# Layer 0's output projection by seven half-size products with positions as rows, in a two-layer mLSTM and gated-attention trunk

## The chip, the cores and the metric

The kernel runs on one core of a Trainium2 chip. The metric is the device time of one execution in microseconds (us). The core's engines each work through a queue of their own in order: TensorE (PE; its weight loads are listed as PEld), VectorE (DVE), ScalarE (ACT), GpSimd (POOL), and SyncE (SP), which here only issues DMAs.

## The reference

512 positions of width 1024 go through two layers, each `x <- x + RMSNorm_post(mixer(RMSNorm_pre(x)))`. Layer 0's mixer is an mLSTM with 4 heads of width 512, layer 1's a gated linear attention with 4 heads. Cut to what matters here:

```python
for i in range(DEPTH):                        # DEPTH = 2
    h = rms_norm(x, pre_norm_w[i])
    out = mlstm_mixer(h, ...) if i == 0 else gla_mixer(h, ...)
    x = x + rms_norm(out, post_norm_w[i])
# the end of mlstm_mixer: y is (512, 2048), w_out is (2048, 1024)
y = (hn * norm_w + skip * uc) * silu(z)
return y @ w_out
```

## The kernel before

Activations lie with channels on the 128 partitions and the 512 positions along the free axis; a tile `t2` is 128x512 float32, and 59 buffers of that size are shared by all of them. Every large product is made in three matmuls: both operands are split into a high part (float32r, a copy by ScalarE) and a low part (the difference, by VectorE), and high x high, high x low and low x high are added up in PSUM. `mm` (L123) issues all matmuls, `split` (L138 high, L139 low) all splits, so the profile is read by tile names.

Weights come in chunks of 128x1024, one DMA on SP's queue into one of three `raw` buffers, then a split into `whi` and `wlo` (four buffers each). `run_jobs` writes out the program: for each job it first forms the chunks of the jobs up to `LA` = 3 ahead, then runs what `later` has put off to this job, then pops `n` entries of the list `steps` (VectorE and ScalarE work spread over the jobs) and `b` of `spare`, and then issues the job's matmuls and what follows them. No planner reorders it: each engine's queue has the order in which this loop comes to its instructions.

Layer 0 has four heads. For head h the weighted scores `S` and values `VS` give the numerators (`m_num`: den and four num banks), then `m_scale`, `m_skip` (GpSimd), `m_rstd` and `m_y` finish y, and `y_split` splits it. The output projection follows: `out_full` and `out_job` take one block of 128 output channels at a time as the stationary side and positions as the moving side, in two halves of 256 positions; eight blocks x two halves x 16 blocks of y x 3 = 768 matmuls of 256 columns. Half 0 is finished first; `residual` then makes its norm factor by a matmul with ones and adds x, `x1_done` applies layer 1's input weight and splits the result into `ghi2` and `glo2`, and a `turn` of four TensorE transposes per pair of blocks stores x1 by rows for the end of the kernel. Layer 1's first five products (`kept_a` for half 0, `kept_b` for half 1) run while half 1's residual steps go on. Since x1 isn't normed yet, every evacuation in layer 1 multiplies by `rs1` or `rcol` (`pre_rstd`, `rstd_columns`).

Layer 1's own output projection is already made of seven half-size products P1 to P7 (Winograd's form of Strassen's method): positions are the stationary side in blocks of 128, 512 output channels the moving side. Its sums of weight blocks U, W, Z and R are made in DRAM by 32 DMAs of GpSimd's queue, `combine` makes the sums of y blocks, and 336 matmuls of 512 columns do the work. P3 and P7 come already split from DRAM (`PRE`).

## Time and profile before

| | |
|---|---|
| runs before | 917.6 us median of 3 (916.42 to 917.76) |
| the profiled execution | 917.5 us, its span 915.8 us |
| TensorE busy | 902.4 us (99%), 4624 matmuls |
| VectorE, ScalarE, GpSimd busy | 630.6, 523.3, 183.2 us |
| mean granted TensorE clock | 0.996 of full |
| DMA | 147.58 MB, mean 161 GB/s |

The span runs from the first to the last instruction of the core. Busy times of matmuls overlap, since one starts before the record of the one in front has ended; VectorE's and ScalarE's overlap by less.

### The profile page before, as it was taken

The page shows a single profiled execution, that of the slowest core. Times are in us where ns is not written, and L with a number is a line of the kernel's source. Part 1 is how long each engine was busy: PE and PEld are TensorE (multiplying, and loading weights), DVE is VectorE, ACT ScalarE, POOL GpSimd, SP SyncE. Part 2 cuts the span into 40 slices and gives each one's busy share as a digit, 9 for nine tenths or more (in the row PEclk, how much of TensorE's full clock was granted, in tenths as well). Part 3 has the DMA queues.
Part 4 walks back from the last instruction along what each step waited for, and adds up shares of the span by engine and source line. Part 5 has one row for each costly group of instructions (what it writes and reads, how often), then busy time and mean ns, then how long its engine had stood idle before and what let it go on. Part 6 is the DMA issues. An engine that isn't in the chain of part 4 may idle for free. (4 is left out here: it accounts for less than half of the span.)

```text
span 915.8 us, 12449 instructions
## 1 busy us (share of the span) xinstructions
PE 902.4 (99%) x4624; PEld 760.7 (83%) x4624; DVE 630.6 (69%) x916; ACT 523.3 (57%) x885; POOL 183.2 (20%) x162
## 2 busy tenths in 40 slices
PE   9999999999999999999999999999999999999995
PEld 6887878878877888899999997777888888888874
DVE  5999797886886668788658746743346547478854
ACT  6865685756654558866557626544435345365642
POOL 0022552262250043245002310421000000000121
PEclk9999999999999999999999999999999999999998
DMA  8334344352342223222775694995343736383776
GB/s 309 120 122 147 117 151 137 116 169 97 123 142 69 93 70 115 92 93 69 232 235 198 206 323 166 236 243 140 116 138 114 242 115 200 118 287 104 269 275 138
DMA packets 50882, 147.58 MB, mean 161 GB/s; under 512 B 5792, under 2 KB 10272, under 8 KB 50528
## 3 DMA queue, kind: packets, MB, share of 16 engines
q1 hardware_dynamic: 44832, 120.29, 39.7%
q0 software_dynamic: 5696, 26.22, 10.8%
q8 instruction: 38, 0.62, 0.3%
q14 instruction: 28, 0.23, 0.1%
q10 hardware_dynamic: 288, 0.22, 0.1%
HBM read 129.92 MB, written 34.60 MB: 180 GB/s over the span
## 5 line engine op out<-in xcount | busy, mean ns | idle before, releaser
L139 DVE TENSOR_TENSOR wlo<-raw,whi 128x1024 fp32r<-128x1024 f32 (+1 forms) x146 | 186.3, 1284 | 98.8 <-ACT whi L138 98.1
L138 ACT CAST whi<-raw 128x1024 fp32r<-128x1024 f32 (+1 forms) x146 | 149.9, 1036 | 79.0 <-PE gv L123 24.2
L394 POOL TENSOR_TENSOR vp<-V,wv 128x512 f32<-128x512 f32 x56 | 88.6, 1604 | 177.4 <-ACT V L482 92.6
L123 PE MATMUL op<-yhi,whi 128*128 128x256 f32 x256 | 73.5, 287 | 0.0
L123 PE MATMUL op<-yhi,wlo 128*128 128x256 f32 x256 | 72.5, 283 | 0.4 <-DVE wlo L139 0.4
L123 PE MATMUL op<-ylo,whi 128*128 128x256 f32 x256 | 72.8, 284 | 0.0
L397 DVE SCALAR_TENSOR_TENSOR vp<-V,wv 128x512 f32<-128x512 f32 x72 | 68.0, 987 | 0.0
L163 POOL DMA_DIRECT2D whi<-wpP x8 | 4.3, 536 | 244.7 <-DMA raw<-in_w_gout 216.9
L123 PE MATMUL gz<-g2h,whi 128*128 128x512 f32 x128 | 51.5, 403 | 0.5 <-PEq L1156 0.5
L123 PEld LDWEIGHTS op<-ylo,whi 128*128 128x128 f32 x256 | 49.1, 192 | 1.1 <-DVE ylo L139 0.6
L123 PE MATMUL gz<-g2h,wlo 128*128 128x512 f32 x128 | 49.9, 390 | 0.0
L123 PE MATMUL gz<-g2l,whi 128*128 128x512 f32 x128 | 49.8, 389 | 0.0
L123 PE MATMUL qk<-chi,whi 128*128 128x512 f32 x128 | 49.8, 389 | 0.0
L123 PE MATMUL qk<-chi,wlo 128*128 128x512 f32 x128 | 49.8, 389 | 0.0
L123 PE MATMUL qk<-clo,whi 128*128 128x512 f32 x128 | 49.8, 389 | 0.0
L123 PE MATMUL gv<-whi,g2h 128*128 128x512 f32 x128 | 49.8, 389 | 0.0
L123 PE MATMUL gv<-wlo,g2h 128*128 128x512 f32 x128 | 49.8, 389 | 0.0
L123 PE MATMUL gv<-whi,g2l 128*128 128x512 f32 x128 | 49.8, 389 | 0.0
L123 PEld LDWEIGHTS op<-yhi,wlo 128*128 128x128 f32 x256 | 49.1, 192 | 0.6 <-DVE wlo L139 0.6
L123 PEld LDWEIGHTS op<-yhi,whi 128*128 128x128 f32 x256 | 49.1, 192 | 0.5 <-issue 0.5
L123 PE MATMUL z<-hhi,whi 128*128 128x512 f32 x112 | 44.1, 394 | 0.0
L123 PE MATMUL z<-hlo,whi 128*128 128x512 f32 x112 | 43.7, 390 | 0.0
(286 smaller groups left out, 2503.9 us busy)
## 6 DMA issues: line engine op xcount, KB each, us to landing
raw<-in_w_min SPq DMA_DIRECT2D x30, 512.0 KB, 3.7
raw<-in_w_mout SPq DMA_DIRECT2D x29, 512.0 KB, 4.2
wv<-in_wgv SPq DMA_DIRECT2D x32, 256.0 KB, 3.6
raw<-in_w_qk SPq DMA_DIRECT2D x16, 512.0 KB, 3.7
raw<-in_w_gqk SPq DMA_DIRECT2D x16, 512.0 KB, 4.0
raw<-in_w_gz SPq DMA_DIRECT2D x16, 512.0 KB, 5.2
raw<-in_w_gv SPq DMA_DIRECT2D x16, 512.0 KB, 4.1
raw<-in_w_v SPq DMA_DIRECT2D x8, 512.0 KB, 3.5
```

Source lines behind the costliest of these rows:

```text
L123: nc.tensor.matmul(out, lhsT=lhsT, rhs=rhs, start=start, stop=stop, skip_group_check=more)
L138: nc.scalar.copy(hi, src)
L139: nc.vector.tensor_sub(lo, src, hi.bitcast(F32))
L163: nc.gpsimd.dma_start(to, of)
L394: nc.gpsimd.tensor_mul(j, V[h][i], w)
L397: nc.vector.scalar_tensor_tensor(j, V[h][i], 1.0, w, op0=ALU.mult, op1=ALU.mult, accum_out=o)
```

## The change

Layer 0's output projection is made like layer 1's. A class `Seven` holds the seven products for both (`m7` for layer 0, `g7` for layer 1, whose code is moved into it). Layer 0's weight sums are made by 32 DMAs that GpSimd issues during the q and k products of heads 1 to 3. y of heads 0 and 1 is split as the first operand and saved to DRAM (`ysave`), and loaded again for the combines. Positions are now rows: the post-norm's sum of squares is a free-axis accumulation on ScalarE, the residual comes from x by rows (`xrows`), `h_rows` applies layer 1's input norm by rows, and TensorE turns the normed rows (`turn`) into `ghi2` and `glo2`. As layer 1's input is normed by then, its evacuations lose their multiply: q and k are copied by ScalarE, z goes straight from PSUM into the activation. For head 3 the square sums move from GpSimd to VectorE; `m_skip` stands ahead of `m_num`. Layer 0's products all come as raw chunks (`DMA_LOW` is empty, so the "dma" kind isn't used). The weights of the low-rank gate load earlier, in the same order of jobs.

```diff
+    class Seven:
+        TO = {"P1": "a", "P6": "a", "P7": "a", "P4": "a", "P5": "c", "P3": "c", "P2": "d"}
...
+        def sum_start(self, n, c):
+            w = self.w
+            nc.gpsimd.dma_start(self.wsum[n, c], {"U": w[1, 0, c], "W": w[0, 0, c], "Z": w[0, 1, c], "R": w[0, 0, c]}[n])
+        def sum_add(self, n, c):
+            w, ws = self.w, self.wsum
+            nc.gpsimd.dma_start(ws[n, c], {"U": w[1, 1, c], "W": ws["U", c], "Z": ws["W", c], "R": w[1, 0, c]}[n],
+                                accum_op=ALU.add, max_dma_last_dim=4096)
...
+        def first_operand(self, k, y):
+            nc.vector.tensor_sub(y[:, self.b], y[:, self.a], y[:, self.b])
+        def combine(self, k):
+            y1, y2 = self.Y[0, k], self.Y[1, k]
+            a, b = self.a, self.b
+            for to, x, y in ((y1[:, b], y1[:, b], y2[:, b]), (y1[:, a], y1[:, b], y1[:, a]),
+                             (y2[:, a], y1[:, b], y2[:, a])):
+                nc.vector.scalar_tensor_tensor(to, x, -1.0, y, op0=ALU.mult, op1=ALU.subtract)
+        def operand4(self, c):
+            self.ops["4", c] = t2("yhi", F32R), t2("ylo", F32R)
+            for i in range(2):
+                split(*(z[:, HALF[i]] for z in self.ops["4", c]), self.Y[1, 2 * c + i][:, self.a])
...
+        def product(self, name, chunks, tb, c0=0):
+            to = self.TO[name]
+            if (to, tb) not in self.bank:
+                self.bank[to, tb] = psum("op")
+            ps = self.bank[to, tb]
+            more = name in ("P6", "P7", "P4", "P3")
+            for c, (whi, wlo) in enumerate(chunks):
+                for i in range(2):
+                    k = 2 * (c0 + c) + i
+                    yh, yl = (z[:, tb * P:(tb + 1) * P] for z in self.block(name, k))
+                    mm(ps, yh, whi[i], k == 0 and not more, False, more)
+                    mm(ps, yh, wlo[i], False, False, more)
+                    mm(ps, yl, whi[i], False, k == 7, more)
...
+        def out_part(self, r, m, to, name, tb):
+            self.parts[r, m] = t2("o")
+            nc.vector.tensor_add(self.parts[r, m], self.bank[to, tb], self.sums[name, tb])
+            self.part_sum(r, m, self.parts[r, m])
...
+    m7, g7 = Seven("m", w_mout, 0), Seven("g", w_gout, 1, PRE)
...
+    m_sums = sums_of(m7)
+    def next_sums(n):
+        for _ in range(n):
+            if m_sums:
+                m_sums.pop(0)()
     A = [None] * NH
     V = [None] * NH
     st = {}
@@ -517,6 +690,7 @@
                     gate_add(wgr[:, 16 * which + n, :], *d[n])
             later(2 if h else 3, gates)
+            next_sums(3 if h else 0)
...
-                nc.gpsimd.tensor_add(sqs[0], sqs[0], sqs[vt])
+                (nc.vector if h == NH - 1 else nc.gpsimd).tensor_add(sqs[0], sqs[0], sqs[vt])
...
-            if vt < 2:
-                load_uc(n + 2)
-            nc.gpsimd.tensor_mul(zs[n], st["uc", n], zs[n])
+            nc.gpsimd.tensor_mul(st["uc", n], st["uc", n], zs[n])
...
+    ysave = dp.tile([8, P, T], F32, name="ysave")
+    def y_out(h, vts):
         for vt in vts:
-            n = 4 * h + vt
-            yhi[n], ylo[n] = t2(f"yhi{n}", F32R), t2(f"ylo{n}", F32R)
-            split(yhi[n], ylo[n], HC[h][vt])
+            n, y = 4 * h + vt, HC[h][vt]
+            if h < 2:
+                m7.first_operand(n, y)
+                m7.operand("1", n, y)
+                nc.sync.dma_start(ysave[n], y)
+            else:
+                m7.Y[1, n - 8] = y
+                m7.operand("2", n - 8, y)
+    def load_y(k):
+        m7.Y[0, k] = t2("yr")
+        nc.sync.dma_start(m7.Y[0, k], ysave[k])
...
+        if h == NH - 1:
+            job(lambda: [load_y(k) for k in range(4)], n=0)
+        job(lambda h=h: (m_skip(h), m_num(h), m_scale(h)), n=0)
...
-                for n in range(2):
-                    out_full(n)
+                for c in range(2):
+                    m7.job("P1", c)
+                    m7.job("P5", c)
...
+    def x1_rows(r):
+        c = m7.row_rstd(r)
+        for m in range(2):
+            o = m7.parts[r, m]
+            nc.vector.scalar_tensor_tensor(o, o, c, m7.pw[:, m * T:(m + 1) * T], op0=ALU.mult, op1=ALU.mult)
+        for m in range(2):
+            o = m7.parts[r, m]
+            nc.vector.tensor_add(o, o, m7.res[r, m])
+            m7.part_sum(r, m, o, ssx)
+            nc.sync.dma_start(x1_d[r, :, m * T:(m + 1) * T], o)
+    def h_rows(r):
+        c = m7.row_rstd(r, ssx, rsx1)
+        for m in range(2):
+            hrow[r, m] = t2("hr")
+            nc.scalar.activation(hrow[r, m], m7.parts[r, m], AF.Copy, scale=c)
...
+    def turn(kp, half):
         sl = HALF[half]
+        ps = psum("xt")
         for i in range(2):
             k = 2 * kp + i
+            for j in range(2):
+                nc.tensor.transpose(ps[:, (2 * i + j) * P:(2 * i + j + 1) * P],
+                                    hrow[2 * half + j, k // 4][:, k % 4 * P:(k % 4 + 1) * P], ident)
...
+            of, w = ps[:, HALF[i]], col(PV_PRE + 8 + k)
+            nc.scalar.activation(ghi2[k][:, sl], of, AF.Identity, scale=w)
+            nc.vector.scalar_tensor_tensor(glo2[k][:, sl], of, w, ghi2[k][:, sl].bitcast(F32),
+                                           op0=ALU.mult, op1=ALU.subtract)
...
+    def m_after_p7():
+        for tb in range(2):
+            m7.out_part(tb, 1, "a", "e5", tb)
+        later(1, lambda: (x1_rows(0), x1_rows(1)))
+        later(2, lambda: (h_rows(0), h_rows(1)))
...
+    job(lambda: (m7.load_pw(0), steps.extend(pairs(m7.combine, (0, 2)))), n=0)
+    DK = lambda name, c: "dma" if (name, c) in DMA_LOW else "ring"
+    m7.job("P5", 2)
+    job(lambda: (head_steps(NH - 1), [load_y(k) for k in range(4, 8)], steps.extend(
+        pairs(m_op3, (0,)) + [lambda v=v: (m_y(NH - 1, (v, v + 1)), y_out(NH - 1, (v, v + 1))) for v in (0, 2)]
+        + pairs(m_op3, (2,)) + pairs(m7.combine, (4, 6)) + pairs(m_op3, (4, 6))
+        + [lambda c=c: m7.operand4(c) for c in range(4)]
+        + [lambda: None, lambda: gla_weights(0, 0)] + [lambda: None] * 6
+        + [lambda i=i: gla_weights(i // 2 + 1, i % 2) for i in range(4)])), n=0)
+    for name, c in (("P5", 3), ("P1", 2), ("P1", 3), ("P3", 0), ("P3", 1), ("P2", 0), ("P2", 1), ("P6", 0), ("P6", 1),
+                    ("P3", 2), ("P3", 3), ("P6", 2), ("P6", 3), ("P2", 2), ("P7", 0), ("P7", 1)):
+        m7.job(name, c, kind=DK(name, c))
+    job(lambda: [m7.load_res(r, rows_of_x) for r in (0, 1)], n=0)
+    for name, c in (("P7", 2), ("P7", 3), ("P2", 3)):
+        m7.job(name, c, la=LA + (name == "P2"), kind=DK(name, c))
+    job(lambda: [m7.load_res(r, rows_of_x) for r in (2, 3)], n=0)
+    def m_last(r):
+        m7.parts[r, 1] = t2("o")
+        nc.vector.tensor_copy(m7.parts[r, 1], m7.bank["a", r - 2])
+        m7.part_sum(r, 1, m7.parts[r, 1])
+    for c in range(4):
+        m7.job("P4", c, n=2, kind="t2r" if c > 1 else "ring")
+    for kp in range(4):
+        job(lambda kp=kp: turn(kp, 0), n=0, la=0)
+    job(lambda: (m_last(2), x1_rows(2), m7.product("P4", m7.last, 1)), n=8)
...
-        return lambda: nc.vector.tensor_mul(raw[j][:, sl], ps, rs1[:, sl])
+        return lambda: nc.scalar.copy(raw[j][:, sl], ps)
...
-    job(lambda: pre_rstd(0), n=0)
-    kept_a(*head[0], "keep")
-    job(lambda: (rstdB(), steps.extend([lambda k=k: addB(k) for k in range(KP + 2)])), n=0)
+    kept_a(*head[0], "keep", 4)
+    job(lambda: (m_last(3), x1_rows(3), h_rows(2)), n=0)
     kept_a(*head[1], "keep")
+    job(lambda: h_rows(3), n=0)
     kept_a(*head[2], "keep2")
-    job(lambda: low_rank(0), n=2)
+    job(lambda: low_rank(0))
     kept_a(*head[3], "keep2", 1)
     kept_a(*head[4], "keep2", 0)
     job(lambda: low_rank_evac(0), n=8, la=0)
+    for kp in range(4):
+        job(lambda kp=kp: turn(kp, 1), n=0, la=0)
+    kept_b(*head[0])
     job(lambda: low_rank(1), la=0)
-    kept_b(*head[0])
-    job(lambda: pre_rstd(1))
+    kept_b(*head[1])
```

## Rows read from the trace of the kernel before

**Rows 1.** Windows: stretch, busy PE, PEld, DVE, ACT, POOL, clock, DMA, GB/s.

```profile
541.00:637.00 96.00, 95.48 (x408) 74.83 (x407) 52.88 (x97) 47.52 (x68) 19.34 (x34) 1.00 0.81 216
828.00:906.00 78.00, 77.37 (x340) 63.10 (x339) 56.58 (x95) 40.24 (x74) 12.09 (x20) 1.00 0.64 200
```

**Rows 2.** Waits of TensorE, whole span: us in total, times, longest.

```profile
PE op L123 <- DMA wlo<-wpP: 0.6, 1, 0.6
```

**Rows 3.** Tile op (both layers' outputs): count, ns min/median/max, first and last start.

```profile
L123 PE MATMUL op<-yhi,whi x256: 277/283/683, 396.7 to 500.6; 128*128 128x256 f32 x128
...
L123 PE MATMUL op<-whi,yhi x96: 388/389/793, 828.0 to 894.5; 128*128 128x512 f32 x96
```

**Rows 4.** Timeline of TensorE, layer 0's output stage: start, us, instruction, [idle before].

```profile
396.72 0.68 PE L123 MATMUL op<-yhi,whi 128*128 128x256 f32 x1
...
408.63 0.39 PE L123 MATMUL den<-shi,csr 128*128 128x512 f32 x1
...
417.52 0.33 PE L123 MATMUL op<-yhi,whi 128*128 128x256 f32 x1
...
501.38 1.13 PE L123 MATMUL ssq<-sq,cs 128*128 128x256 f32 x4 [0.21 <-POOL sq L310]
502.34 0.60 PE L898 MATMUL xt<-cs,o 128*128 128x128 f32 x4
```

**Rows 5.** Timeline of TensorE, layer 1's output stage.

```profile
839.40 0.79 PE L123 MATMUL op<-whi,yhi 128*128 128x512 f32 x1
840.04 0.40 PE L123 MATMUL op<-wlo,yhi 128*128 128x512 f32 x1
...
905.89 0.39 PE L123 MATMUL op<-khi,ylo 128*128 128x512 f32 x1
```

**Rows 6.** Timeline of VectorE around the start of layer 0's output.

```profile
404.84 1.29 DVE L739 TENSOR_TENSOR hc<-hc,z 128x512 f32<-128x512 f32 x2
406.05 1.22 DVE L139 TENSOR_TENSOR wlo<-raw,whi 128x1024 fp32r<-128x1024 f32 x1
407.18 2.73 DVE L666 SCALAR_TENSOR_TENSOR vlo<-V,vmean,vhi 128x512 fp32r<-128x512 f32 x4
...
423.79 0.69 DVE L737 TENSOR_TENSOR hc<-hc,rs 128x512 f32<-128x512 f32 x1 [1.51 <-ACT rs L729]
```

**Rows 7.** Timeline of VectorE, one combine of two blocks in layer 1's stage.

```profile
841.85 0.42 DVE L1251 SCALAR_TENSOR_TENSOR pt<-pt,pt 128x256 f32<-128x256 f32 x1
...
844.11 1.22 DVE L139 TENSOR_TENSOR wlo<-raw,whi 128x1024 fp32r<-128x1024 f32 x1
```

**Rows 8.** Timeline of VectorE behind P7 of layer 1's stage.

```profile
895.35 0.69 DVE L1324 TENSOR_TENSOR o<-op,e 128x512 f32<-128x512 f32 x1 [0.67 <-PE op L123]
...
899.84 0.15 DVE L1330 TENSOR_TENSOR rso<-ssq 128x1 f32<-128x1 f32 x1
900.59 1.42 DVE L1340 SCALAR_TENSOR_TENSOR o<-o,rso,pw 128x512 f32<-128x512 f32 x2 [0.60 <-ACT rso L1332]
```

**Rows 9.** Timeline of ScalarE behind P7 of layer 1's stage.

```profile
896.13 0.63 ACT L1314 ACTIVATE sq<-o 128x512 f32<-128x512 f32 x1 [0.69 <-DVE rso L1330]
```

**Rows 10.** Timeline of ScalarE, two high halves of layer 1's input.

```profile
481.88 0.90 ACT L885 ACTIVATE g2h<-o,pv 128x256 fp32r<-128x256 f32 x2
```

**Rows 11.** Timeline of ScalarE in layer 0's output stage, a late raw chunk.

```profile
439.18 1.05 ACT L138 CAST whi<-raw 128x1024 fp32r<-128x1024 f32 x1 [4.14 <-DMA raw<-in_w_mout]
```

**Rows 12.** Windows behind the last product, columns as in rows 1.

```profile
906.00:909.00 3.00, 0.28 (x2) 0.00 (x0) 1.36 (x3) 1.19 (x4) 0.00 (x0) 1.00 1.14 257
909.00:912.00 3.00, 0.00 (x0) 0.00 (x0) 0.81 (x2) 0.00 (x0) 0.00 (x0) 0.52 1.02 382
```

**Rows 13.** Timeline of TensorE at the kernel's start.

```profile
1.58 3.71 PE L123 MATMUL warm<-warm 128*128 128x512 f32 x9 [1.58 <-DVE warm L289]
5.39 0.51 PE L123 MATMUL u<-ghi,whi 128*128 128x512 f32 x1
```

**Rows 14.** DMA issues: tile, queue, count, KB each, median us to landing.

```profile
raw<-in_w_mout SPq DMA_DIRECT2D x29, 512.0 KB, 4.2
```

More of the change, by code (lines that the diff above doesn't have):

```diff
@@ new lines, in m_after_p2 @@
+    def m_after_p2():
+        for tb in range(2):
+            later(2, lambda tb=tb: m7.out_part(2 + tb, 0, "d", "e1", tb))
+    m7.after = {"P1": lambda: m7.keep_copy("e1", "a"), "P5": lambda: m7.keep_copy("e5", "c"),
+                "P6": lambda: (m7.keep_copy("u2", "a"), m_after_p3()), "P2": m_after_p2, "P7": m_after_p7}
+    pairs = lambda f, ks: [lambda k=k: (f(k), f(k + 1)) for k in ks]
+    m_op3 = lambda k: m7.operand("3", k, m7.Y[0, k])
+    job(lambda: (m7.load_pw(0), steps.extend(pairs(m7.combine, (0, 2)))), n=0)
@@ L1096, in tile_mlstm_gla @@
     kept_b(*head[4])
-    job(rstd_columns)
     def full_qk(w, j, after):
@@ L1270, in tile_mlstm_gla @@
-    bank, sums, parts = {}, {}, {}
-    def product(name, to, chunks, tb, c0=0):
-        if (to, tb) not in bank:
-            bank[to, tb] = psum("op")
-        ps = bank[to, tb]
-        for c, (whi, wlo) in enumerate(chunks):
-            for i in range(2):
-                k = 2 * (c0 + c) + i
-                yh, yl = (z[:, tb * P:(tb + 1) * P] for z in block(name, k))
-                more = name in ("P6", "P7", "P4", "P3")
-                mm(ps, yh, whi[i], k == 0 and not more, False, more)
-                mm(ps, yh, wlo[i], False, False, more)
-                mm(ps, yl, whi[i], False, k == 7, more)
@@ L1285, in tile_mlstm_gla @@
-    last = [None] * 4
-    TO = {"P1": "a", "P6": "a", "P7": "a", "P4": "a", "P5": "c", "P3": "c", "P2": "d"}
-    def prod_job(name, c, n=1, la=LA):
-        def run(chunk):
-            for tb in range(2):
-                product(name, TO[name], [chunk], tb, c)
-            if c == 3:
-                AFTER[name]()
-        job(run, chunk_of(name, c), n=n, la=la)
-    def keep_copy(name, to):
-        for tb in range(2):
-            sums[name, tb] = t2(name)
-            nc.scalar.copy(sums[name, tb], bank[to, tb])
@@ L1322, in out_part @@
[L1322 to L1333 removed]
+                    job(lambda i=i: [g7.operand("1", k, g7.Y[0, k]) for k in range((0, 2, 5)[i - 1], (2, 5, 8)[i - 1])], n=0)
@@ L1373, in tail_y @@
         for k in (4 + v, 5 + v):
-            operand("2", k, Y[1, k])
+            g7.operand("2", k, g7.Y[1, k])
     for c in range(4):
-        prod_job("P1", c)
-        prod_job("P5", c)
+        g7.job("P1", c)
+        g7.job("P5", c)
         if c == 0:
-            job(lambda: steps.extend([lambda k=k: (combine(k), combine(k + 1)) for k in (0, 2)]), n=0)
+            job(lambda: steps.extend(pairs(g7.combine, (0, 2))), n=0)
         if c == 1:
```

385 lines of the change are left out of this document (150 added, 235 removed).

## Prediction

> **What bounds the kernel now.** I read the busy times by stretch first, then TensorE's waits, then its starts one by one, and last the queues of VectorE and ScalarE around the stage that changes. In [rows 1] TensorE is busy for 95.48 of 96.0 us behind the stage that changes and for 77.37 of 78.0 in layer 1's own, and its longest wait after the start is 0.6 us [rows 2]: the kernel lasts as long as TensorE's queue. So a change is worth the TensorE time that it removes, less the waits that it makes. The time per matmul must be read from starts, though. The 256-column products of layer 0's output have a median of 283 ns and the 512-column ones of layer 1's 389 [rows 3], but their records overlap. From the stage's first product at 396.72 to the sum of squares behind its last at 501.38 it is 104.66 us [rows 4]; den and num of head 3 take 8.89 of them (408.63 to 417.52) and two sums of squares 0.8, so 768 products take 95.0 us, 0.124 each. Layer 1's stage has 336 products of 512 columns from 828.0 to 905.89 and one step of 0.23, 78.1 us; without its sum of squares (0.45) and two hitches (0.41 at 839.40 [rows 5], 0.8 at the wait of [rows 2]) 76.4 us, 0.2275 each.
>
> The page "Trace Analysis" of the Trainium skill (Identifying the Most-Contended Engine) says that a matmul's busy time is no measure of TensorE's use, since the records are pipelined; by busy time this change would save 768 x 0.283 - 336 x 0.389 = 87 us, by starts 18.6, and the starts add up to the span.
>
> **What TensorE is relieved of.** 768 half-width products (95.0) give way to 7 x 4 chunks x 2 x 3 x 2 = 336 full-width ones, at layer 1's pace 76.4. The ones-matmuls of the residual's and the next norm's sums go: twelve, the first four 0.96 (501.38 to 502.34 [rows 4]), all by their starts 2.3. So do the four transposes of rstd_columns, 0.35 (the four of xt show 0.60 with their overlap [rows 4]). Thirty-two transposes of x1 stay thirty-two. Saved: 95.0 + 2.3 + 0.35 - 76.4 = **21.2 us**. The evacuations of layer 1 that lose their multiply (gqk, gz, gv, low rank) save nothing: TensorE doesn't wait there [rows 1, 2].
>
> **What VectorE and ScalarE get to do in a shorter stage.** A chunk of weights now feeds 12 products, 2.73 us, and each still needs a high half on ScalarE and a low half on VectorE, formed three chunks ahead. VectorE, by starts: low half 1.13, a 512-wide operation 0.605 (two in 1.21), four vlo 2.65 [rows 6], a combine of two blocks 2.26 (841.85 to 844.11 [rows 7]). Going are the 256-wide square sums and residual multiplies of half 0; coming are four pairs of combines, eight third operands, out_part, x1_rows and, for head 3, the additions of the squares.
>
> The first place where it binds is the start of the stage. VectorE ends m_y of head 2 at 406.05 and only then reaches the low half of the fourth chunk; it is done at 407.2. TensorE wants it at 396.72 + 3 x 2.73 = 404.9: 2.3 late. From 406.05 to the low half of the seventeenth chunk VectorE has, in the order of the job list: fourteen low halves 15.8, vlo 2.65, m_y of head 2 2.4, its four operands 2.4, ad 0.6, three square sums 1.8, m_scale 2.7, rs 0.7, combines 9.0, third operands 4.9, m_y of head 3 4.8 and its operands 2.4: 50.2 us. To these come waits on ScalarE: for rs (1.51 at 423.79 [rows 6], and now a high half of 0.95 stands behind Ln and Exp), and 0.5 before each of the two operand pairs of head 3: 3.5. End: 406.05 + 53.7 = 459.8. TensorE wants that chunk after 16 jobs, num and a sum of squares: 396.72 + 43.7 + 8.9 + 0.5 = 449.8. So **10.0 us** of waits, spread over the jobs P5 chunk 1 to P6 chunk 2; behind them VectorE needs 1.8 per job of 2.73 and is no longer late. Bounds: with no wait on ScalarE 6.5, with layer 1's own excess 1.2; upward, all waits doubled, 13.5.
>
> **The turn.** Layer 1's first product needs the normed rows of half 0, turned. Call E the end of P7. TensorE then has P2 chunk 3 (2.73) and P4 for row block 2 (24 products, 5.46): 8.2 us of cover. The chain is: second out_part 0.6 [rows 8], its square 0.63 [rows 9] and the reading of its sum; four 512-wide low halves of P4's chunks stand in front of x1_rows, E+4.1. Row 0: sum to scale 0.75 (899.84 to 900.59), two scalings 1.3 [rows 8], two additions 1.2: E+7.4. Its last square ends at E+8.2 on ScalarE; only behind it stand row 1's Ln and Exp, E+8.8; scalings and additions, E+11.4; squares, E+12.1. Then h_rows on ScalarE: Ln and Exp 0.5 and two copies 1.1 for row 0, 0.5 and one copy 0.6 for row 1: E+14.8. The first transpose takes blocks of both rows. So TensorE stands **6.6 us**. Bounds: 4.2, if the low halves in front had been done sooner; 8, if the raw chunks of P4 come late.
>
> Behind the turn TensorE has 1.4 of transposes and 5.5 of P4 for block 3, until E+21.7. ScalarE still owes two squares 1.6, two kept chunks 2.0, one more 1.1 and the low-rank weights 2.0, and only then, from E+21.7, the eight high halves that layer 1 starts from, 0.45 each (two in 0.90 [rows 10]) against 0.36 of matmuls for each. The last comes at E+25.3, its low half 0.5 later; layer 1's first job ends some **1.6** late.
>
> The idle before the turn should also bring the clock down. After the kernel's last product, at 906, the granted clock is 1.00 until 909 and 0.52 in the 3 us behind that [rows 12]: idle took it to the lower level, 1.2 GHz. How long it stays there under work no row tells; the nearest are the nine warm-up matmuls behind the empty start, 3.81 us from 1.58 to 5.39 [rows 13], 0.42 each instead of 0.2275. If 3.8 us behind the turn run at half pace, P4's last block ends 1.9 later; ScalarE's debt of 1.6 lies behind the same matmuls, so **0.3** of it counts. Bounds 0 and 1.9. The page "TensorE: Matmul & The Clock Gate" (Why this matters for your kernels) warns of idle gaps between bursts of matmuls, which speaks against this change; the end of this trace agrees with it (0.52).
>
> For half 1 the same eight follow the second turn: its rows are ready near the time TensorE reaches them, and the pace costs **1.5** again. Both between 0 and 4.
>
> **Queues.** SP gets 16 loads and stores of ysave, eight of xrows, eight stores of x1 and pw; each stands in front of later weight loads. One such wait is in the stage before: ScalarE waited 4.14 for a raw chunk at 439.18 [rows 11], under cover of three chunks. GpSimd gets 32 issues of weight sums beside v_gate's products, whose readers are two jobs (10.9 us) away; I cost these at nothing, and if a product is late by more, ScalarE stands with the high halves behind it: 0 to 4.
>
> **Sum.** The profiled execution took 917.5 us (span 915.8 and 1.7 around it; the median of the runs is 917.6). 917.5 - 21.2 + 10.0 + 6.6 + 1.6 + 0.3 + 1.5 = **916.3 us**. What TensorE saves is waited away, nearly all of it. Of such a kernel 0.2% (1.8 us) can be told from no change: faster is below 915.8, slower above 919.4.
>
> **Rivals.** *The queues keep up, as in layer 1.* Its stage has nearly this order of steps, and VectorE, busy 56.58 of 78 us [rows 1], let TensorE wait 1.2. Against: there two of the seven products come already split, and four chunks are formed ahead at its start. With 1.2 for 10.0: 907.2. Chance 0.25.
>
> *No wait at all*, the turn covered too: 917.5 - 21.2 = 896.3. It needs the chain to be 6.6 shorter; 0.04.
>
> *SP's queue becomes the bound* (slower). A load of y or of x rows waits for one of the 59 shared buffers, with the raw chunks behind it. From the moment that VectorE is late there is no chunk in hand, and each such wait counts in full: 4.1 by [rows 11], two of them 8.2: 924. It decides from one wait of 3.5 us upwards; for it, about 21 MB in some 90 us; against it, the three raw buffers and landings of 4.2 us [rows 14]. Chance 0.18.
>
> *The clock stays low for longer behind the turn* (slower). Between the two turns TensorE has P4's last block and some 17 us of layer 1's half-width products. If it takes 10 us of work at half pace, not 3.8, to bring the level back, 5.0 is lost where 1.9 was counted, and ScalarE's debt covers none of the rest: 919.4. It decides from there on; [rows 13] speak against it, since the warm-up came back in 3.81. Chance 0.08.
>
> **How the numbers follow.** Forecast: 0.45, 911 to 920, by the bounds of its waits, the start of the stage above all. The others 0.25, 0.04, 0.18, 0.08. Faster is the first two rivals and near two fifths of the forecast, 0.46; same a good third of the forecast, 0.17; slower the rest, 0.37. From 904 to 926 no more than 2 in 10 is left out.
>
> **What would show it.** Right: P products in 336 records with starts 0.227 apart; gaps of TensorE that end on VectorE's wlo, 2 to 3 us each, from the fourth product job to about the twelfth, 8 to 13 in all; one gap of 5 to 8 us before the first transpose, ended by ScalarE's copy of the second row block, with the clock low behind it; nothing new from the gate projections on. Wrong, to the fast side: the stage within 2 us of 76.4 plus num; to the slow side: gaps that end on a DMA of raw, or a granted clock below 1.0 outside the turn.

## The result, and the profile after

The changed kernel takes 973.68 us (median of 4 runs, 971.75 to 974.76) beside 917.44 for the kernel before on the same chip: ratio 1.0613, 95% interval 1.0591 to 1.0634. The forecast was 916.3. The profiled execution has a span of 972.9 us.

First TensorE's waits over the whole span, in the columns of [rows 2], where the longest after the start was 0.6 us.

```profile
PE op L124 <- ACT whi L139: 13.0, 2, 10.3
PE xt L1002 <- ACT hr L993: 11.1, 4, 6.7
PE ssq L124 <- POOL sq L872: 5.0, 2, 4.5
PE gacc L124 <- DVE qkl L140: 4.5, 4, 1.9
PE op L124 <- ACT khi L139: 4.2, 1, 4.2
PE gz L124 <- ACTq L1272: 3.7, 1, 3.7
PE op L124 <- DVE wlo L140: 2.0, 5, 0.5
```

TensorE's queue no longer sets the time; the first six groups of waits do, and the low clock behind them. Of these only the second (the turn) was forecast in kind, and its size is met by luck, as shown below. The waits on VectorE's low half, to which the forecast gave most of its 10.0 us, have 2.0.

The other way to read two traces of the same order is by starts of the same work. The first z product behind the q/k stage stands 8.5 us later than before, the first product of layer 0's output 17.0 (413.71 against 396.72 of [rows 4]), the first product of layer 1's scores 49.6, the first gv product behind the branch 54.1. From there to the end it is 3 more (1.8 in layer 1's own output stage, 1.1 behind its last product), which no experiment followed up. So there are four main places, and three of them lie outside the stage that the forecast worked out:

- the q/k stage of layer 0, 8.5
- the heads' num and z stage, a further 8.5
- the output stage and the junction of the layers, 32.6, where the forecast had a gain of 1.2
- from the scores to the first gv product, across the branch in layer 1, 4.5

**The output stage.** Windows of the changed kernel (columns as in [rows 1]):

```profile
413.00:437.00 24.00, 23.48 (x117) 19.73 (x118) 20.96 (x27) 20.45 (x30) 9.59 (x3) 1.00 0.58 197
437.00:462.00 25.00, 19.69 (x73) 14.20 (x72) 17.98 (x29) 9.13 (x14) 11.10 (x18) 0.90 0.88 303
462.00:486.00 24.00, 13.27 (x40) 9.45 (x40) 12.03 (x20) 8.89 (x14) 0.00 (x0) 0.67 0.66 231
486.00:510.00 24.00, 23.62 (x103) 18.92 (x103) 19.62 (x30) 14.55 (x26) 0.00 (x0) 1.00 0.65 208
```

The first stretch, where VectorE was to begin to be late, is nearly full. In the second the DMA engines are busy for 0.88 at 303 GB/s, and in the third TensorE, VectorE and ScalarE are busy for only 13.3, 12.0 and 8.9 of 24 us: they wait for data. The mean clock falls to 0.90 and 0.67. Behind the waits of 2.78, 10.26 and 4.20 us in this stage TensorE runs at the lower of its levels, 1.2 GHz (granted 0.50), and its products start 0.43 us apart instead of 0.2275:

```profile
478.33 0.63 PE L124 MATMUL op<-wlo,yhi 128*128 128x512 f32 x1
478.76 0.63 PE L124 MATMUL op<-whi,ylo 128*128 128x512 f32 x1
```

By the starts this costs 8.4 us in the stage, beside 21.2 us of waits. What the engines wait for, ScalarE's timeline shows; [rows 11] has one such wait, of 4.14:

```profile
456.67 1.04 ACT L139 CAST whi<-raw 128x1024 fp32r<-128x1024 f32 x1 [6.23 <-DMA raw<-in_w_mout]
...
473.25 1.04 ACT L139 CAST whi<-raw 128x1024 fp32r<-128x1024 f32 x1 [10.24 <-DMA raw<-in_w_mout]
```

The DMA view of 437 to 462 (queue, packets, MB, share; then issues, KB each, median us to landing) names the traffic:

```profile
q0 software_dynamic: 366, 6.26, 72.3%
q1 hardware_dynamic: 455, 1.29, 14.9%
...
wsgU<-in_w_gout POOLq DMA_DIRECT2D x4, 512.0 KB, 6.0
...
raw<-in_w_mout SPq DMA_DIRECT2D x2, 512.0 KB, 19.4
yr<-ysave SPq DMA_DIRECT2D x4, 256.0 KB, 27.2
```

Raw chunks land in 19.4 us instead of the 4.2 of [rows 14], behind copies of layer **1**'s weights (wsg), which GpSimd issues. Its timeline, and then that of the kernel before:

```profile
427.50 13.35 POOL L890 TENSOR_TENSOR ucr<-ucr,z 128x512 f32<-128x512 f32 x4 [14.41 <-DMA ucr<-uc_d]
440.80 2.00 POOL L454 DMA_DIRECT2D wsgU<-in_w_gout  x4
442.77 1.92 POOL L454 DMA_DIRECT2D wsgR<-in_w_gout  x4
```
```profile
522.41 1.29 POOL L310 TENSOR_TENSOR sq<-sq 128x512 f32<-128x512 f32 x1 [2.16 <-ACT sq L307]
523.63 2.19 POOL L1059 DMA_DIRECT2D wsU<-in_w_gout  x4
```

In the program these copies stand behind layer 0's stage in both kernels. Before, GpSimd's square sums of x1 stood in front of them in its queue, the last at 522.41. The change moved these sums to ScalarE, and GpSimd, with nothing left to wait for, issues the copies 83 us earlier.

**The heads.** ScalarE in head 1, at the place where TensorE then waits 4.5 us for the square sums:

```profile
366.03 0.62 ACT L139 CAST yhi<-hc 128x512 fp32r<-128x512 f32 x1 [4.09 <-DVE hc L477]
367.80 0.62 ACT L139 CAST yhi<-hc 128x512 fp32r<-128x512 f32 x1 [1.15 <-DVE hc L477]
...
371.81 2.05 ACT L870 ACTIVATE sq<-num 128x512 f32<-128x512 f32 x4
```

For each block of y of heads 0 and 1 VectorE now makes the first operand (a subtraction), ScalarE its high half, VectorE its low half, and only then comes the next subtraction: 1.77 us a block. The squares of num stand behind all four.

**The turn** is as forecast in kind: TensorE idles from 526.5 to 533.16, then once more, and the clock is low behind it (0.50 from 533 to 538).

```profile
511.71 0.39 PE L124 MATMUL op<-whi,yhi 128*128 128x512 f32 x1
...
521.52 0.50 PE L124 MATMUL op<-khi,yhi 128*128 128x512 f32 x1 [4.20 <-ACT khi L139]
...
526.11 0.39 PE L124 MATMUL op<-khi,ylo 128*128 128x512 f32 x1
533.16 0.48 PE L1002 MATMUL xt<-cs,hr 128*128 128x128 f32 x1 [6.67 <-ACT hr L993]
534.95 2.39 PE L1002 MATMUL xt<-cs,hr 128*128 128x128 f32 x10 [1.31 <-ACT hr L993]
```

That the first gap is 6.67 for a forecast of 6.6 is luck. P7 ends at the first line shown (E of the forecast). The copy of the second row block, which ends the second gap, comes 23.2 us later, where the forecast's chain had 14.8; but TensorE had 14.6 us to do instead of 8.2, since P4 waited 4.20 us for its weights and then ran at the low clock. The two errors cancel in part.

### The profile page after: what moved, and what is told of

Read it like the earlier page. It is cut to its first block, busy times and chain, and to the rows that moved or that the text cites. A ratio compares the mean times of both kernels' runs of the same rounds, so it can differ in the third digit from the quotient of the medians.

```text
span 972.9 us, 11621 instructions
## 1 busy us (share of the span) xinstructions
PE 909.6 (93%) x4176; PEld 739.6 (76%) x4176; DVE 639.8 (66%) x930; ACT 536.4 (55%) x930; POOL 196.4 (20%) x185
## 5 line engine op out<-in xcount | busy, mean ns | idle before, releaser
L139 ACT CAST whi<-raw 128x1024 fp32r<-128x1024 f32 (+1 forms) x143 | 147.1, 1037 | 101.0 <-PE gv L124 29.5
L124 PE MATMUL op<-whi,yhi 128*128 128x512 f32 x200 | 82.2, 411 | 13.2 <-ACT whi L139 13.0
L124 PE MATMUL op<-wlo,yhi 128*128 128x512 f32 x200 | 81.4, 407 | 3.4 <-DVE wlo L140 2.0
L124 PE MATMUL op<-whi,ylo 128*128 128x512 f32 x200 | 79.9, 399 | 0.0
L407 DVE SCALAR_TENSOR_TENSOR vp<-V,wv 128x512 f32<-128x512 f32 x72 | 74.6, 1076 | 1.3 <-DMA wv<-in_wgv 1.3
L124 PEld LDWEIGHTS op<-whi,yhi 128*128 128x128 f32 x200 | 38.9, 194 | 23.6 <-ACT whi L139 14.2
L164 POOL DMA_DIRECT2D whi<-wpgP x8 | 4.3, 537 | 251.2 <-DVE pt L1291 221.6
L890 POOL TENSOR_TENSOR ucr<-ucr,z 128x512 f32<-128x512 f32 x16 | 35.6, 2255 | 91.5 <-DMA ucr<-uc_d 91.5
L124 PEld LDWEIGHTS op<-wlo,yhi 128*128 128x128 f32 x200 | 38.8, 194 | 16.5 <-DVE wlo L140 5.6
L124 PEld LDWEIGHTS op<-whi,ylo 128*128 128x128 f32 x200 | 38.9, 194 | 7.9
```

What stands on the lines that cost most here:

```text
L124: nc.tensor.matmul(out, lhsT=lhsT, rhs=rhs, start=start, stop=stop, skip_group_check=more)
L139: nc.scalar.copy(hi, src)
L164: nc.gpsimd.dma_start(to, of)
L407: nc.vector.scalar_tensor_tensor(j, V[h][i], 1.0, w, op0=ALU.mult, op1=ALU.mult, accum_out=o)
L890: nc.gpsimd.tensor_mul(st["uc", n], st["uc", n], zs[n])
```

## The experiments

Each kernel ran beside the kernel before on the same chip. The starts are us later than in the kernel before, from the traces: first z product behind the q/k stage, first product of layer 0's output, first of layer 1's scores, first gv product. They come from one profile each: in the six kernels that change nothing ahead of the first z product (changed, e1, e2, e4, e5, e7) the first column runs from 7.5 to 10.7, so differences of 3 us between starts mean little. The medians are of the timed runs.

```
kernel    z     output  scores  gv     median  ratio (95%)
changed   8.5   17.0    49.6    54.1   973.7   1.0613 (1.0591-1.0634)
e1        8.7   17.3    34.3    36.5   958.2   1.0454 (1.0416-1.0493)
e2       10.7   18.8    53.9    56.2   975.1   1.0630 (1.0612-1.0648)
e3        0.4   16.6    50.0    52.3   972.3   1.0601 (1.0581-1.0621)
e4        7.5   16.9    49.5    53.3   973.8   1.0619 (1.0600-1.0637)
e5       10.4   16.0    48.2    52.3   970.3   1.0549 (1.0515-1.0584)
e6        4.8   14.0    46.8    51.1   972.8   1.0605 (1.0587-1.0624)
e7        9.3   17.0    29.5    34.8   955.9   1.0416 (1.0395-1.0436)
e8        5.4   11.1    22.4    26.9   947.5   1.0325 (1.0303-1.0346)
e9        0.1    1.5    17.8    20.1   941.1   1.0267 (1.0246-1.0288)
e10       0.3    1.5    24.8    28.4   948.3   1.0346 (1.0321-1.0370)
e11      -0.3   -0.4    15.5    15.2   932.2   1.0162 (1.0144-1.0180)
e12       1.1    1.8    17.9    17.4   938.7   1.0224 (1.0200-1.0248)
e13       0.1    2.5    15.8    15.3   936.7   1.0206 (1.0192-1.0220)
e14       0.4    3.1    16.0    15.8   936.5   1.0209 (1.0193-1.0226)
e15       0.9    3.6    14.0    13.4   932.7   1.0165 (1.0149-1.0180)
e16       0.2    2.9    17.2    16.6   936.1   1.0209 (1.0193-1.0224)
e17      -0.2   -0.2    12.0    11.7   927.0   1.0098 (1.0081-1.0114)
e18       9.6   19.4    41.4    45.8   966.8   1.0523 (1.0497-1.0550)
```

**e1, layer 1's sums held back.**

```
+    hold = cp.tile([P, 1], F32, name="hold")
-    job(lambda: spare.extend(sums_of(g7)), n=0)
+    job(lambda: (nc.gpsimd.tensor_copy(hold, rsx1[:, 3:4]), spare.extend(sums_of(g7))), n=0)
```

> Only a GpSimd copy of one column, which needs the last norm of layer 0's rows, is put in front of layer 1's 32 weight-sum transfers; nothing else moves. Theory (the sums run ahead at 441 us and their transfers delay the raw chunks of layer 0's output stage, which land in 19 to 24 us instead of 4.2): raw chunks of the stage land in 3 to 6 us throughout, the TensorE waits of 2.9 and 10.7 us on ScalarE's high half and 4.2 us on the kept chunk go, the stage from its first product to the first product of layer 1's scores is 13 to 20 us shorter, and the time falls from 973.7 to 954 to 961. Rival (the order of VectorE's and ScalarE's queues sets the stage, as the forecast's first term had it): the waits return on VectorE's low half, the stage is less than 5 us shorter, the time stays at 969 or more.

The copies go out at 551.14, and between the output's start and the scores 15.7 us are gone. GpSimd's timeline and a row of the DMA view of 437 to 462 in this kernel:

```profile
551.02 0.18 POOL L1225 COPY hold<-rsx 128x1 f32<-128x1 f32 x1 [109.86 <-ACT rsx L569]
551.14 1.99 POOL L454 DMA_DIRECT2D wsgU<-in_w_gout  x4
```
```profile
raw<-in_w_mout SPq DMA_DIRECT2D x2, 512.0 KB, 4.3
```

Raw chunks are back at 4.3 us; the theory held. (A further 2.3 us went at the branch, which this edit doesn't touch: see e12.)

**e11, the same burst put into the kernel before**, which has nothing else of the change.

```
         job(lambda h=h: (m_num(h), m_scale(h), m_skip(h),
+                         [wsum_start(n, c) for n in "URWZ" for c in range(4)] if h == NH - 1 else None), n=0)
...
-    job(lambda: spare.extend([lambda n=n, c=c: wsum_start(n, c) for n in "URWZ" for c in range(4)]
-                             + [lambda n=n, c=c: wsum_add(n, c) for n in "URWZ" for c in range(4)]), n=0)
+    job(lambda: spare.extend([lambda n=n, c=c: wsum_add(n, c) for n in "URWZ" for c in range(4)]), n=0)
```

> The kernel before, in which the 16 copies of layer 1's weight sums are issued by GpSimd right behind the skip products of head 3, at about 425 us, and not behind the square sums at 523 us; the 16 additions stay where they were. Theory (the burst of transfers delays the raw chunks of the output stage to some 20 us whatever the kernel): TensorE waits 4 to 12 us in the stage of 396 to 502, time 921 to 930. Rival (only the changed kernel's stage, which uses a chunk in 2.73 us instead of 5.5 or 2.7 and has them formed three ahead, feels it): less than 1.5 us, 916 to 919. The first wait behind the branch is read from the same profile: 0.5 us in the one profile of the kernel before.

15.4 us later at the first transpose, more than expected, and 932.2 us. The cost belongs to the burst, not to the shorter stage. Its DMA view, 427 to 460:

```profile
q0 software_dynamic: 512, 8.39, 74.1%
q1 hardware_dynamic: 781, 2.19, 19.8%
...
raw<-in_w_mout SPq DMA_DIRECT2D x4, 512.0 KB, 17.7
```

**e17 and e18, the same burst in smaller rows.** In e11 the two queues move 512 and 781 packets, of 16 KB and 2.8 KB in the mean. Both kernels add one argument to the copies:

```
+                                max_dma_last_dim=4096)
```

> The kernel of e11 (the kernel before with layer 1's 16 copies issued at 427 us, 932.2) with rows of 4 KB in those copies, as the additions have, instead of 32 KB. The same bytes at the same time. Theory (the DMA engines take a packet from each queue in turn, so a queue with packets of 16 KB gets four times the bytes of one with 4 KB): the raw chunks land in 6 to 10 us instead of 17.7, the loss of 15.3 us in the output stage falls to 0 to 5, the time to 917 to 922. Rival (8.4 MB in flight fill the engines, whatever their packets): chunks still take 14 us or more, time 929 to 934.

> The changed kernel with rows of 4 KB instead of 32 KB in the 32 copies of both layers' weight sums; the order of issue is unchanged, so layer 1's copies still run ahead. Theory (packet size): the waits of 2.9, 10.7 and 4.2 us on ScalarE's high halves in the output stage fall to what they are with the sums held (1.8, 1.2 and 3.1), and the q/k stage loses 4 to 8 instead of 8.5: time 954 to 960. Rival (bytes in flight): 970 to 976.

The same view of e17:

```profile
q0 software_dynamic: 2190, 8.00, 69.8%
q1 hardware_dynamic: 1224, 3.43, 27.2%
...
raw<-in_w_mout SPq DMA_DIRECT2D x7, 512.0 KB, 8.2
```

Chunks land in 8.2 instead of 17.7 us, as expected of the packet theory, but the loss falls only from 15.4 to 11.9: with the 24 products that a chunk feeds in one half in some 3 us, and chunks formed three ahead, 8.2 is still late, now in nine small waits on the two halves (4.0 and 3.4 us) instead of two long ones. In the changed kernel 10.7 us are won from the output's start to the scores (32.6 to 22.0), where holding the sums won 15.7. So packet size is a part of the cause, the bytes in flight the other; both expectations were too narrow. The page "DMA: Bandwidth & Descriptors" of the Trainium skill (SWDGE vs HWDGE vs iDMA) says that each DMA engine goes round its queues and changes over at packet boundaries; the 366 to 455 packets of the changed kernel and the fall in e17 agree with it, though in e17 GpSimd's queue still moves more packets than SP's.

**e3 and e6, layer 0's sums elsewhere**: three a z job, or one in each u (from the fifth), v and q/k job.

```
-            next_sums(3 if h else 0)
+            next_sums(1)          # e6, and the same line in u_job and v_job
+            next_sums(0 if early else 3)    # e3, in z_job
```

> Layer 0's 32 weight-sum transfers are issued three per z projection (11 of those jobs, 282 to 395 us of the changed kernel) instead of three per q/k projection job of heads 1 to 3. Theory (in the q/k stage they keep the DMA engines 0.91 to 0.96 busy and stand between GpSimd's gate products, and cost 8.5 us of TensorE): the 8.5 us to the first z product behind the q/k stage are gone, to within 1 us. What the z stage then loses is open: nothing if its DMA share of 0.23 to 0.29 leaves room (time 965), the same 8 us again if GpSimd's square sums or the raw chunks are delayed there (time 973). Rival (something else in the q/k stage costs the 8.5 us): they stay.

> Layer 0's 32 weight-sum transfers are issued one in each u (from the fifth on), v and q/k projection job, from about 40 to 240 us, instead of three in each q/k job of heads 1 to 3. Theory (the cost is that of bursts which fill the DMA engines; 32 transfers take about 60 us of all 16 engines, and there is room for that beside 0.4 of share if they are spread): the first z product behind the q/k stage comes 6 to 8.5 us earlier and nothing is given back behind it, 965 to 968. Rival (every transfer costs TensorE the same wherever it lies, through GpSimd's gate products or VectorE's): the loss of 8 us is spread, and the time stays at 971 to 975.

The 8.5 us at the first z product go in e3 (0.4 left), and come back by the output's start (16.6). In e6 some 5 us are lost at the very start: with nothing ahead of them GpSimd issues the first three at 1.33 us, among the first loads of x. That is the mechanism of e1 once more. From there to the first z product e6 loses nothing. The line is GpSimd's of e8, which has this edit too:

```profile
1.33 1.68 POOL L454 DMA_DIRECT2D wsmU<-in_w_mout  x3 [0.80 <-POOLq L1485]
```

**e2 and e5, the two orders in the heads**: GpSimd's skip products back behind the square sums; all first operands before the splits.

```
-        job(lambda h=h: (m_skip(h), m_num(h), m_scale(h)), n=0)
+        job(lambda h=h: (m_skip(h), m_num(h), m_scale(h)) if h == NH - 1 else (m_num(h), m_skip(h), m_scale(h)), n=0)
...
+        if h < 2:
+            for vt in vts:
+                m7.first_operand(4 * h + vt, HC[h][vt])
```

> Only the order on GpSimd for heads 0 to 2: the products of the skip path go back behind the square sums of the same head, as in the kernel before. Theory (the products wait for their reloaded operand and take 8 us a head, with the square sums queued behind them, and TensorE waits for those sums): the wait of 4.5 us before head 1's sum of squares and the 1.4 us at head 0 go, layer 0's output stage starts 6 to 8 us earlier, the time falls to 965 to 968. Rival (GpSimd needs the same time in either order, and what is behind is then late): the start of the output stage moves by less than 2 us, or m_y waits for the skip products instead.

> Only the order of eight blocks of y of heads 0 and 1: the four subtractions on VectorE that make the first operands come first, then the four splits, instead of subtraction, high half, low half for one block after the other. Theory (in the changed kernel each subtraction waits behind the low half of the block before, and that behind ScalarE's high half: 1.77 us a block, four in a row, with ScalarE's squares of num, GpSimd's additions of them and TensorE's sum of squares behind them): the wait of 4.5 us before head 1's sum of squares falls below 1, the squares of head 1 start 4 to 5 us earlier behind num, the output stage starts 4 to 7 us earlier, the time falls from 973.7 to 967 to 970. Rival (GpSimd's skip products, which slow VectorE's neighbours from 0.4 to 1.5 us, make the wait): it stays above 3 us.

Each alone wins little: the wait before head 1's sum of squares is 4.6 us in e2 and 2.4 in e5, and the theories' times are missed, by 7 us and by 0.3. From the first z product to the output's start the changed kernel loses 8.5, e2 8.1, e5 5.6. In e2 ScalarE still goes back and forth with VectorE; in e5 GpSimd's products run beside VectorE's subtractions and slow them (four in 2.52 us, for 0.42 each). Both together (e9, e12) lose 1.4 and 0.7: one chain with two causes, and either alone keeps most of it. (e9 and e12 also spread layer 0's sums; e6, which does that alone, loses 9.2 here.)

**e7, the low-rank loads off SP's queue**, on top of e1.

```
-                    nc.sync.dma_start(gur[16 * g6:16 * (g6 + 1), :], w_gu[:, j * T:(j + 1) * T])
+                    nc.gpsimd.dma_start(gur[16 * g6:16 * (g6 + 1), :], w_gu[:, j * T:(j + 1) * T])
```

> With layer 1's sums held as in the first experiment (958.2), the 13 small loads of the gate's low-rank weights are issued by GpSimd instead of SP. Theory (each takes SP's queue 0.57 us, 7 us in all at 491 to 498, and five loads of x rows behind them 2.3 more; the raw chunk of P4 behind these is what ScalarE waits 4.4 us for): P4's raw chunks are issued 6 to 7 us earlier, the TensorE wait of 3.1 on the high half goes and the first transpose comes 3 to 4.5 us earlier behind P7, time 953 to 955. Rival (the row sums behind P7 set the turn whatever P4 does): the 3.1 go, the wait at the turn grows by as much, and the time stays at 957 to 959.

At the scores 4.8 us are won (34.3 to 29.5): the wait of 3.1 on P4's high half is gone, the one at the transposes grows from 6.6 to 8.1. The 2.3 us in the time are fewer, because the stretch across the branch takes 3.2 more here; 955.9 lies between the theory and the rival, and the intervals of e1 and e7 overlap, so the gain in the time is not told from noise.

**e8, e9, e12, e13: together.** e8 is hold, pace, first operands and loads; e9 paces from head 1 on (the remainder one a z job) and puts the skip products behind; e12 moves the branch; e13 has the skip products ahead again for head 2.

> Layer 1's sums held, layer 0's paced one a job, the first operands together, and the low-rank loads issued by GpSimd. If the four places add up: 958.2 less 7 (paced), 5 (first operands) and 4 (loads) is 942, between 937 and 946. By the forecast (every queue beside VectorE's and ScalarE's costed at nothing) this is the kernel that it described: 916. What lies between the two is the forecast's waits mis-sized: the stage, the turn or the half behind it, to be read from TensorE's gaps.

> The kernel of e8 with two edits: layer 0's sums are issued one a job only from head 1 on (no earlier than GpSimd's gate products of head 0, behind which they stand), and for heads 0 to 2 GpSimd's skip products go behind the square sums. In e8 GpSimd, with nothing to wait for, issued its first sums at 1.3 us, among the first loads of x, and TensorE stood 4 us at 6 to 10 us. Theory (GpSimd's queue runs ahead wherever nothing in it waits): the start is again that of the changed kernel, 5.3 us earlier than in e8; of the 2.5 us before head 1's sum of squares 1 to 2 go; the time is 939 to 943. Rival (the q/k stage pays again when the same sums lie in a shorter stretch): 944 to 948.

```
-    job(branch)
     gz_job(3)
+    job(branch)
```

> The kernel of e9 with the branch behind the fourth gz projection instead of ahead of it. Theory (TensorE itself stands at the branch, because what follows has to be fetched): a gap of 2 to 5 us goes with the branch to the first gv product, the time stays within 2 us of e9. Rival (the fourth gz projection waits for a bank or an operand that ScalarE gives free only behind the branch): the gap falls under 1 us and the time is 2 to 5 us below e9.

> The kernel of e12 (938.7) with GpSimd's skip products ahead of the square sums again for head 2, as in the changed kernel; behind them for heads 0 and 1 only. Theory (in e9 and e12 the products of head 2 came late for VectorE's m_y, and the low half behind it was 3.6 us late at the start of the output stage): the den of head 3 is 4 to 6 us earlier than in e12, the time 933 to 935. Rival (VectorE has the same work before the fourth low half anyway, as the forecast's first term had it): 937 to 939.

e8 missed its bounds by 1.5 us, through the 5.3 at the start. e9 fell in its bounds, and shows the forecast's first term where it was put: with the skip products of head 2 behind the sums, VectorE's timeline of e9 is that of [rows 6],

```profile
408.16 1.29 DVE L913 TENSOR_TENSOR hc<-hc,ucr 128x512 f32<-128x512 f32 x2
409.37 1.22 DVE L140 TENSOR_TENSOR wlo<-raw,whi 128x1024 fp32r<-128x1024 f32 x1
```

and TensorE waits 2.2 us for that half. In e13 they are ahead, the den of head 3 comes 2.8 us earlier, and the time is 936.7, 1.7 above the theory's bounds; its interval overlaps that of e12.

In e12 the gap at the branch is gone (0.15 us), and the time is 2.5 below e9, as the rival had it. In e4 the gz projections leave their bank through VectorE again:

```
+                if n < 4:
+                    nc.vector.tensor_copy(zs[n], ps)
```

> The first four gz projections of layer 1 leave their bank by a VectorE copy, with Silu in place behind it, as many instructions as in the kernel before; nothing else changes. Theory (the bank of the product behind the branch was last read by ScalarE, and TensorE's wait for it reaches across the branch, until ScalarE has passed it): the gap of 4.1 us behind the branch falls to 0.5 to 1, the time to 969 to 970. Rival (TensorE itself waits for the instructions behind the branch): the gap stays at 3.5 to 4.5 and the time at 973 to 974.

The gap stayed (2.8), so that bank isn't the cause. In all changed kernels that kept the branch there TensorE waited 2.3 to 3.7 us at the fourth gz; in the kernel before it waited 0.5, in e11 and e17 0.3. e12 shows that the place of the branch decides, but it doesn't rule out the fetching of what follows. In e9 TensorE runs one product behind the branch and then stands, and the profile shows nothing that it waits for:

```profile
654.26 0.47 PE L124 MATMUL gz<-g2h,whi 128*128 128x512 f32 x1
657.20 0.50 PE L124 MATMUL gz<-g2l,whi 128*128 128x512 f32 x1 [2.46 <-issue]
```

What it waits for is not settled.

**e10, e14, e15, e16: the junction.**

```
+        later(1, lambda: [x1_rows(r, c) for r, c in [(r, m7.row_rstd(r)) for r in (0, 1)]])   # e10, e15
...
+            if m:                                                                            # e10, e15
+                nc.vector.tensor_scalar_mul(hrow[r, m], m7.parts[r, m], c)
...
+    job(lambda: (m_last(3), x1_rows(3), h_rows(2), h_rows(3)), n=0, la=0)                     # e10
     kept_a(*head[0], "keep", 4)
...
+    for name, c in (("P7", 2), ("P7", 3), ("P2", 2), ("P2", 3)):                              # e14, e15
...
+                                    m7.res[2 * half + j, k // 4][:, k % 4 * P:(k % 4 + 1) * P], ident)   # e16
```

> The kernel of e9 with the order of the two turns changed: for the first pair of row blocks both row scales are made before the first scaling, of each normed row block ScalarE makes one half and VectorE the other; for the second pair the last row block is copied, scaled and normed right behind P4, ahead of the kept chunks' halves. Theory (each turn waits for a chain of small steps that go back and forth between ScalarE and VectorE): the first gap of 8 us before the transposes falls to 4.5 to 6, the two gaps of the second turn (1.6 and 2 to 4) to under 2 in all, and the time is 6 to 9 us below e9. Rival (the weights of the kept chunks, formed on the same two engines, are then as late as the rows were): 0 to 3 us below e9.

> The kernel of e13 with the third chunk of P2 moved from ahead of P7 to behind it: TensorE has 2.73 us more to do between the end of P7 and the first transpose. Theory (the chain from P7's sums to the normed rows has a fixed length of 16 to 17 us): the first gap falls by 2.7 us, the time by 2 to 3 below e13. Rival (the chunk's halves on ScalarE and VectorE lie in front of the chain and push it back, or P7 now comes too soon for its operands): within 1 us of e13.

> The kernel of e14 with the first pair's part of the reordering of e10 alone: both row scales before the first scaling, half of each normed row block on VectorE. Theory (a chain that goes back and forth): another 1.5 to 2.5 us off the first gap and off the time, while the second turn stays as it was. Rival (what VectorE makes of the rows it can't form of weights): within 1 us of e14, a new gap behind the turn.

> The kernel of e13 in which the 32 transposes read the residual's rows of x, loaded long before, instead of the normed rows of x1, which are still made: the residual sum and the norm ahead of layer 1 are left out of what layer 1 reads, and no transpose waits for them. All other work is the same. Theory (both turns cost what TensorE waits there, some 8 + 3 and 1.5 + 4 us, with the low clock behind the first): the time falls by 13 to 18 us, to 917 to 921. Rival (ScalarE and VectorE have so much to do between the layers that the halves behind the turn come no sooner): a fall of less than 8.

e16 leaves out of what layer 1 reads the residual sum and the norm, so that no transpose waits. It is the telling one. TensorE no longer waits for normed rows, and nothing is won. Its waits between 485 and 545, then those of e13, which it was made from:

```profile
PE gqk L124 <- ACT g2h L1014: 13.4, 2, 9.8
PE gqk L124 <- DVE g2l L1015: 1.8, 2, 1.6
PE xt L1007 <- ACT qkraw L1147: 1.1, 1, 1.1
```
```profile
PE xt L1007 <- ACT hr L998: 11.7, 4, 7.3
PE gqk L124 <- ACT g2h L1014: 1.1, 1, 1.1
PE gqk L124 <- DVE g2l L1015: 0.4, 1, 0.4
```

The transposes run at 492.43, 7.3 us earlier, and the first product of layer 1 waits 9.8 us for ScalarE, whose timeline in e16 shows the high half behind the whole queue of squares, scales, copies and kept halves:

```profile
498.90 0.61 ACT L550 ACTIVATE sq<-o 128x512 f32<-128x512 f32 x1
...
505.24 0.53 ACT L1093 CAST wrst<-wgrr 128x64 fp32r<-128x64 f32 x3
...
509.14 0.46 ACT L1014 ACTIVATE g2h<-xt,pv 128x256 fp32r<-128x256 f32 x1
511.84 0.84 ACT L1014 ACTIVATE g2h<-xt,pv 128x256 fp32r<-128x256 f32 x2 [2.24 <-DVE g2l L1015]
```

So the wait of the transposes isn't what the junction costs: the high halves stand in ScalarE's queue behind the chain of row sums and scales, which e16 still makes, and behind the kept halves. e16 doesn't tell these two apart. Once begun, the eight high halves take 7.5 us here and 7.4 in e13, with waits for VectorE's low halves between them. It fits that more cover (e14) won nothing (the wait went to P4's high half, 4.1 us), that the reordering of both turns (e10) lost 7 us (5.0 on kept halves, 4.0 on the low-rank rows), and that e15, which takes one stall out of the chain and shares one of its steps between the two engines, won 3.8 over e14, the one gain of the four that is clear of noise. Its edit to `h_rows` shares that step for the second pair of row blocks too, which the expectation had left as it was, so the gain may not be the first turn's alone.

## Why the prediction was wrong, by its steps

- **Bound, and what TensorE is relieved of: right.** The products start 0.227 apart wherever none waits and the clock is full.
- **Queues, "I cost these at nothing": the step that failed.** GpSimd's queue was looked at for whom its new work delays, not for what its lost work had held back. The square sums that left it were the only thing in front of layer 1's copies: 15.7 us by e1, 15.4 by e11 in the kernel before. Layer 0's own 32 transfers, allowed 0 to 4, cost 8.5 in the q/k stage (0.1 in e9). SP's queue, a rival at 924, showed too (4.8 at the scores by e7), but through 13 small loads of the gate's weights, which take its time; whether loads of y or x rows that wait for a buffer cost anything, as the rival had it, no run shows.
- **What VectorE and ScalarE get to do: the heads were left out.** The first operands of heads 0 and 1 are among what comes, ahead of the stage, and were in no sum; with GpSimd's new order they cost 7 to 8 (e9, e12 against the changed kernel).
- **Start of the stage, 10.0:** met in size once the queues are mended, but partly by luck. From the stage's first product to the last ahead of the transposes e8 takes 407.77 to 497.92, 90.15 us; 312 products at 0.2275, num 8.89 and a sum 0.45 are 80.3: 9.8 of waits. In e13 it is 12.7. Of the kind that the forecast had, ended by VectorE's low half, are only 2.2 in e8, 3.3 in e13 and 4.5 in e9; 3.0 in e8 end on ScalarE's high half.
- **The turn, 6.6 + 1.6 + 0.3:** right in kind, short in size. In e13 it is 19.3 us from the last product to the first of layer 1 (492.23 to 511.54), less 6.9 of transposes and P4: 12.4 for 8.5. From the end of P7 the second row block is there after 17.4 us (14.8 forecast), the first high half starts after 24.0 (21.7) and the last ends after 31.4 (25.3). Both the chain and the pace of the halves were priced too low, and the wait of the transposes, to which the forecast gave 6.6, is not what decides (e16).
- **Half 1, 1.5:** from there to the scores e13 takes 73.1 us where the kernel before took 66.1 with some 2 us more of TensorE's work in it: about 9. Recorded waits are 4.6 of them, 3.1 before the second turn; the rest is not taken apart.
- **The low clock:** foreseen at the turn alone (0.3). In the changed kernel it came behind the stage's own waits as well and cost 8.4 there. The prediction had named a clock below 1.0 outside the turn, and gaps that end on a raw chunk, as signs of the slow side; both came.
- **Branch:** not foreseen; 4.5, cause open.
- **A slip in a rival:** with 1.2 for 10.0 the sum gives 907.5, not 907.2; nothing hangs on it.

The sum for the changed kernel at the gv product: 17.0 ahead of the stage, 32.3 of waits and low clock in it (112.6 us less 80.3), 10.8 at the turn, 10.5 behind it, 4.5 at the branch, less 21.2: 53.9 against 54.1 measured. Even the best version, e15, is 1.65% slower than the kernel before; none beat it.

## What to carry to other kernels

When work leaves an engine's queue, ask what stood behind it: a transfer that waits for nothing goes out as soon as its queue is free, and may meet the loads of an earlier stage. Give bulk transfers a data wait of their own where they must not run ahead (here one column copied, 15.7 us), and keep their packets small (4 KB instead of 16 won back 3.5 us of 15.4 in e17). And where a stage gets shorter, take the waits out of its successor one at a time in the trace: in a chain on two in-order engines, removing the wait that is shown may only show the next (e14, e16).

## What the runs showed of the hardware

- Two DMA queues with packets of some 17 KB and 2.8 KB in the mean moved 366 and 455 packets in 25 us, and so 4.9 to 1 in bytes; a chunk of 0.5 MB took 19.4 us instead of 4.2. With smaller packets in e17 it was 2190 to 1224 packets and 8.2 us.
- After standing for 10.26 us TensorE came back at a granted clock of 0.50, and its 512-column products started 0.43 us apart instead of 0.2275.
- VectorE's subtraction of two 128x256 operands took 0.42 us, but 1.51 while GpSimd multiplied (364.49 in the changed kernel), and GpSimd's own four products took 13.35 us at 427.50 and 7.0 before. The "GPSIMD Engine Reference" of the Trainium skill (Specifications) says that GpSimd's access is shared with VectorE's instructions that read two operands from SBUF, and the trace agrees.
